# Sums of a pair's weights by GpSimd, one cut of 64 and 192 columns in every group, and two edits at the end, in a one-core encoder layer

## Chip, core and metric

The kernel runs on one core of one Trainium2 chip. Its time is the device time of one execution in microseconds (us); lower is better. The engines are TensorE (PE in the profile; its weight loads are listed apart as PEld), VectorE (DVE), ScalarE (ACT), GpSimd (POOL) and SyncE (SP), which here only issues transfers. Each engine works through its own queue in order and waits on semaphores for the others.

## The reference

One encoder layer over 512 positions of width 1024, all in float32: a feed-forward block, a mixing block (a Fourier mixer beside grouped-query attention), a second feed-forward block, and a last norm.

```
x = x + 0.5 * swiglu(rms_norm(x, ffn1_norm), ffn1_w_gate, ffn1_w_up, ffn1_w_down)
h = rms_norm(x, mix_norm);  u = h @ w_in
x = x + concatenate([fourier_mixer(u), gqa_attention(u)]) @ w_out
x = x + 0.5 * swiglu(rms_norm(x, ffn2_norm), ffn2_w_gate, ffn2_w_up, ffn2_w_down)
return rms_norm(x, final_norm)

swiglu(h, w_gate, w_up, w_down) = (silu(h @ w_gate) * (h @ w_up)) @ w_down
```

The feed-forward width is 2752: 21 chunks of 128 columns and a tail of 64. The change lies almost wholly in the two feed-forward blocks; its last two edits are in the end of the second one and in the final norm.

## The kernel before

**Precision.** Every float32 operand is split into a high part in the chip's reduced float32 format and a low part that is the rest: ScalarE casts the high part (`nc.scalar.copy`), VectorE subtracts it from the source (`lows`, line 121, where the profile has it as L122). A product is then three matmuls: high by high, high by low, low by high. `product` (line 158) issues these three where a full 512 columns, or a half of them, are the moving side.

**A feed-forward block** (`ffn`, line 254) takes its 21 chunks in four groups. For each group it first makes the activations and then multiplies them by the down weights (`down`, line 455), adding into x. The first group takes plain products. The three others use `seven` (line 375): the gate chunk and the up chunk of one index j are a *pair*, and the two matrix products of a pair, seen as a product of two by two blocks, are done with seven block products instead of eight. A block product is 12 matmuls with 256 moving columns (4 blocks of the contraction, three matmuls each), issued by `multiply` (line 381, matmul at L390), so a pair is 84 matmuls. In the two blocks there are 35 pairs in six such groups: 6, 6, 5, 6, 6 and 6.

**The weights of a pair** are prepared one pair ahead by `prepare` (line 334). SyncE loads the gate chunk into `raw_g` (2 buffers) and the up chunk into `raw_u` (3 buffers, shared with the raw down weights). With the quarters a11, a12 (in `raw_g`) and a21, a22 (in `raw_u`), each 128 by 512, four sums are formed by `combine` (line 361, L362): s1 = a21 + a22, s2 = s1 - a11, into the tile `s12`, and s3 = a11 - a21, s4 = a12 - s2, into `s34`. `s12` and `s34` have one buffer each. Then the raw gate chunk, `s12`, a22 and `s34` are split in high and low parts, which go into 128 by 1024 slots of one tile, `ring` (12 slots; 7 are used by a pair). A slot is taken again as soon as the block products that read it are done. The list that `prepare` returns is worked off in portions, after the steps of the pair before.

**The steps of a pair** in `seven`, with what follows each of them on other engines:

- step 0 writes the PSUM bank r; ScalarE copies r to p1 (L398)
- step 1 writes the bank p2; VectorE adds p1 (L411)
- step 9 of the pair before adds a22's product to that pair's r; ScalarE copies r (L434), VectorE multiplies by the gated half (L435), ScalarE and VectorE split the result into `at` (L436, L122)
- step 3 writes the bank q; ScalarE copies q to p5 (L398)
- step 4 adds to r, once p1 is copied; ScalarE copies r to u2 (L398)
- step 5 adds to q, once p5 is copied; VectorE adds u2 (L421), ScalarE applies the gate function (L422)
- step 6 adds to r, once u2 is copied; ScalarE copies r (L426), VectorE adds p5 (L427)

**Order.** In the feed-forward blocks the order of TensorE's and SyncE's instructions is the program's. The order on VectorE, ScalarE and GpSimd is chosen by the framework's scheduler when the program is built, and is fixed after that.

**Cut matmuls.** `CUTS` (line 33) names, for each group of `seven`, the matmuls (counted from the group's start) whose 256 columns are issued as two matmuls of fewer columns, with the same weights loaded twice:

```
CUTS = {
    (0, 1): {1: P}, (0, 2): {1: P, 2: P}, (0, 3): {4: P}, (2, 1): {1: HALF // 4}, (2, 2): {1: HALF - HALF // 4}, (2, 3): {2: P},
}
```

P is 128 and HALF is 256. The first number of a key is the block (0 is the first feed-forward block, 2 the second), the second the group.

**The end.** The last three of the eight output chunks of the second block's last group are done by `closing` (line 1280) in two halves of 256 columns (tiles `last`), so that the final norm of the first half can run under the products of the second. `finish` (line 1255) multiplies the chunks of x by the norm's row and sends them out: VectorE does six of the eight, GpSimd does chunks 2 and 3, and those two leave in one transfer issued by ScalarE's queue once both are multiplied. GpSimd otherwise only does small powers for norms, a few copies, and a few transfers.

Of the kernel before, what the change touches and what calls it, by code (L numbers as in the profile page):

```python
# [13 lines left out]
P = 128  # L14
S = 512
D = 1024
KD = D // P
F = 2752
NF = F // P
# [9 lines left out]
PLACES = 7  # L29
HALF = S // 2  # L30
USES = "a11", "a12", "s1", "s2", "s4", "s3", "a22"

CUTS = {
    (0, 1): {1: P}, (0, 2): {1: P, 2: P}, (0, 3): {4: P}, (2, 1): {1: HALF // 4}, (2, 2): {1: HALF - HALF // 4}, (2, 3): {2: P},
}
PIECES = (0, 2, 2, 0, 2, 1, 1)
KH = KD // 2
HI_DVE = ("f0", "f1")
SWAP_DMA = ("q1", "q2", "q3")

# [43 lines left out]
def encoder(ctx, tc, A, out):  # L84
    nc = tc.nc
# [43 lines left out]
        plain.append(plain.pop(i))  # L129
        return plain[-1]  # L130

    def weight_slots():
        return (slot().rearrange("p (a b) -> p a b", b=P) for _ in range(2))

    def raw_tile(src, name, n=KD):
        raw = wp.tile([P, KD, P], F32, tag="raw", name=f"raw_{name}")
# [5 lines left out]
        nc.scalar.activation(lo, asf(hi), AF.Copy, scale=-1.0)  # L142
        nc.gpsimd.dma_start(out=lo, in_=src, accum_op=ALU.add)

    def weights(src, name, n=KD, raw=None, by_dma=False):
        raw = raw or raw_tile(src, name, n)
        hi, lo = weight_slots()
        if name in HI_DVE:
            nc.vector.tensor_copy(hi[:, :n, :], raw[:, :n, :])
        else:  # L150
            nc.scalar.copy(hi[:, :n, :], raw[:, :n, :])  # L151
        if by_dma:
            rest_by_dma(lo, hi, src)
        else:
            lows(lo[:, :n, :], raw[:, :n, :], hi[:, :n, :])
        return hi, lo

    def product(ps, whi, wlo, mhi, mlo, first, last):
        nc.tensor.matmul(ps, whi, mhi, start=first, stop=False)  # L159
        nc.tensor.matmul(ps, whi, mlo, start=False, stop=False)  # L160
        nc.tensor.matmul(ps, wlo, mhi, start=False, stop=last)  # L161

    class Norm:
# [90 lines left out]
    def ffn(norm, after, wgu, wd, wdt, groups, opening, closing):  # L254
# [4 lines left out]
        n_ = norm.n  # L259
        n_plain = len(groups[0])  # L260
        with tc.tile_pool(name=f"act{n_}", bufs=1) as ap, tc.tile_pool(name=f"sums{n_}", bufs=2) as sp:
# [72 lines left out]
            def prepare(j, most=False):  # L334

                g = sp.tile([P, KD * P], F32, tag="raw_g", name=f"raw_g{n_}_{j}")
                u = wp.tile([P, KD * P], F32, tag="raw", name=f"raw_u{n_}_{j}")
                for t, c in ((g, 2 * j), (u, 2 * j + 1)):
                    nc.sync.dma_start(out=t.rearrange("p (a b) -> p a b", b=P), in_=wgu[c])
                a11, a12, a21, a22 = g[:, :S], g[:, S:], u[:, :S], u[:, S:]  # L340
                s12 = sp.tile([P, 2 * S], F32, tag="s12", bufs=1, name=f"s12_{n_}_{j}")
                s34 = sp.tile([P, 2 * S], F32, tag="s34", bufs=1, name=f"s34_{n_}_{j}")
                w = {}

                def both(names, src):
                    hi, lo = (take(most and names[0] != "a11") for _ in range(2))
                    nc.scalar.copy(hi, src)  # L347
                    lows(lo, src, hi)
                    for i, n in enumerate(names):
                        w[n] = tuple(t[:, i * S : (i + 1) * S] for t in (hi, lo))  # L350
                    w[max(names, key=USES.index), "slots"] = hi, lo

                def single(n, src):
                    t = take(False)
                    hi, lo = t[:, :S], t[:, S:]
                    nc.scalar.copy(hi, src)
                    lows(lo, src, hi)
                    w[n] = hi, lo
                    w[n, "slots"] = (t,)

                def combine(out, a, b, op):
                    nc.vector.tensor_tensor(out=out, in0=a, in1=b, op=op)  # L362

                return w, [
                    (both, ("a11", "a12"), g),
                    (combine, s12[:, :S], a21, a22, ALU.add),
                    (combine, s12[:, S:], s12[:, :S], a11, ALU.subtract),
                    (both, ("s1", "s2"), s12),
                    (single, "a22", a22),
                    (combine, s34[:, :S], a11, a21, ALU.subtract),  # L370
                    (combine, s34[:, S:], a12, s12[:, S:], ALU.subtract),
                    (both, ("s3", "s4"), s34),
                ]

            def seven(js, done, cuts):

                done = [done]
                banks = {}
                count = iter(range(84 * NF))

                def multiply(ps, wn, on, w, first):

                    (whi, wlo), (mhi, mlo) = w[wn], (part[on][:, i] for i in range(2))
                    for i in range(KH):
                        ks = slice(i * P, (i + 1) * P)
                        for o, (a, b) in enumerate(((whi, mhi), (whi, mlo), (wlo, mhi))):
                            cut = cuts.get(next(count), HALF)
                            for t in (slice(0, cut), slice(cut, HALF)):
                                if t.start < HALF:
                                    nc.tensor.matmul(  # L390
                                        ps[:, t], a[:, ks], b[:, i, t], start=first and i == 0 and o == 0,
                                        stop=i == KH - 1 and o == 2, skip_group_check=not first,
                                    )
                    give(*w.get((wn, "slots"), ()))

                def kept(ps, n, j):
# [58 lines left out]
            def down(d, group, gi):  # L455

                js = [j for j in group if j != "t"]
                whi, wlo = weights(wd[d][:, js[0] : js[-1] + 1, :], f"dn{n_}_{d}_{gi}", len(js))
                w = wt[d // 4][:, d % 4 * P : (d % 4 + 1) * P]

                def steps(ps, t):
                    for i, j in enumerate(group):
                        h, l = (at[:, where[j], o, t] for o in range(2))
                        first, last = i == 0, i == len(group) - 1
                        if j == "t":
                            nc.tensor.matmul(ps[:, t], w, h, start=first, stop=False)
                            nc.tensor.matmul(ps[:, t], w, l, start=False, stop=last)
                        else:
                            k = j - js[0]
                            product(ps[:, t], whi[:, k, :], wlo[:, k, :], h, l, first, last)  # L470
                        yield

                return steps
# [7 lines left out]
            for gi, group in enumerate(groups):  # L481
                last = gi == len(groups) - 1
                ahead = []
                if gi:
                    rest = seven(range(group[0] + 1, min(group[-1] + 2, NF)), ready, CUTS.get((n_, gi), {}))
# [769 lines left out]
    def finish(c0, c1, row, parts):  # L1255

        t = slice(c0 * P, c1 * P)
        pr = row(c0, c1)
        for ks in parts:
            block = slice(ks[0], ks[-1] + 1)  # L1260
            if ks[0] in by_pool:
                for k in ks:
                    nc.gpsimd.tensor_tensor(out=x[k][:, t], in0=x[k][:, t], in1=n3.rb[:, t], op=ALU.mult)
            else:
                y = xt[:, block, t]
                nc.vector.tensor_tensor(out=y, in0=y, in1=pr[:, t].unsqueeze(1).to_broadcast(list(y.shape)), op=ALU.mult)
            queue = nc.scalar if ks[0] in by_pool else nc.sync
            queue.dma_start(out=out[:, block, t], in_=xt[:, block, t])
# [170 lines left out]
```

## Time and profile before

| | us |
|---|---|
| median of 3 runs | 846.33 |
| lowest and highest | 846.12, 846.79 |
| the profiled execution's own time | 846.22 |
| its span, first to last instruction | 844.4 |
| mean granted TensorE clock | 0.997 |
| PE busy | 835.7 |
| DVE busy | 638.3 |
| ACT busy | 465.2 |
| POOL busy | 33.4 |

The profiled execution's time is 1.8 us longer than its span. In rows of groups, the columns are the line, the engine, the operation, what it writes and reads with shapes, the count, then after a bar the busy time in us and the mean of one in ns, then the idle time before. A matmul's end is modelled by the profiler, so the distance from start to start (or time over count in a stretch) tells the pace of matmuls better than their listed duration, which overlaps with the next.

### The profile page before, as it was taken

What the parts mean: (1) busy time and instruction counts of PE and PEld (TensorE: products, weight loads), DVE (VectorE), ACT (ScalarE), POOL (GpSimd) and SP (SyncE); (2) the same over time, 40 slices, a digit from 0 to 9 for tenths busy, and PEclk for the clock granted to TensorE, in tenths of its full rate; (3) what the DMA queues carried; (4) which work ended last, traced back from release to release, by engine and by line L of the source; (5) the groups of instructions that cost most, each with busy time, mean ns of one, the idle gap of its engine ahead of it and who ended that gap; (6) DMA issues with size and microseconds to landing.
All of it is one profiled execution on the core that took longest, in us unless ns stands there. A gap on an engine that the chain in (4) does not pass through costs nothing.

```text
span 844.4 us, 13712 instructions
## 1 busy us (share of the span) xinstructions
PE 835.7 (99%) x5441; PEld 756.4 (90%) x5441; DVE 638.3 (76%) x1007; ACT 465.2 (55%) x781; POOL 33.4 (4%) x35
## 2 busy tenths in 40 slices
PE   9999999999999999999999999999999999999996
PEld 6878998899989998889988888899989998899986
DVE  6997895489757847699998478999945895489453
ACT  7764664167424744677776347657632664157352
POOL 0110000000000000222000000100000000000002
PEclk9999999999999999999999999999999999999998
DMA  7664322323243123414110223543232322323213
GB/s 250 168 141 160 135 89 76 119 101 138 75 137 104 53 65 104 150 50 138 32 69 26 101 74 113 119 171 130 87 110 110 119 89 75 119 100 116 67 45 99
DMA packets 31424, 89.25 MB, mean 106 GB/s; under 512 B 3712, under 2 KB 9344, under 8 KB 31232
## 3 DMA queue, kind: packets, MB, share of 16 engines
q1 hardware_dynamic: 28320, 82.87, 29.0%
q0 software_dynamic: 2496, 4.99, 3.2%
q8 instruction: 42, 0.69, 0.3%
q10 hardware_dynamic: 544, 0.52, 0.2%
q14 instruction: 22, 0.18, 0.1%
HBM read 83.91 MB, written 2.10 MB: 102 GB/s over the span
## 4 chain that ended last, share of the span: by engine, by line
PE 97%; DVE 1%; DMA 0%; issue 0%; ACT 0%; POOL 0%; POOLq 0%; DVEq 0%; ACTq 0%
PE r L390 23%; PE q L390 11%; PE dn L161 8%; PE dn L160 8%; PE dn L159 8%; PE p L390 6%; PE mix L159 4%; PE mix L161 3%; PE mix L160 3%; PE gu L640 3%; PE gu L159 2%; PE gu L161 2%; PE gu L160 2%; PE mix L1130 2%; PE mix L1087 2%; PE mix L936 1%
## 5 line engine op out<-in xcount | busy, mean ns | idle before, releaser
L390 PE MATMUL r<-rt,ring 128*128 128x256 f32 x1687 | 211.1, 277 | 0.0
L390 PEld LDWEIGHTS r<-rt,ring 128*128 128x128 f32 x1687 | 201.9, 188 | 1.1
L161 PE MATMUL dn<-at,ring 128*128 128x512 f32 x300 | 116.9, 390 | 0.5 <-DVE ring L122 0.5
L160 PE MATMUL dn<-at,ring 128*128 128x512 f32 x300 | 116.8, 389 | 0.0
L159 PE MATMUL dn<-at,ring 128*128 128x512 f32 x300 | 116.7, 389 | 0.0
L390 PE MATMUL q<-rt,ring 128*128 128x256 f32 x840 | 107.2, 277 | 0.0
L476 DVE SCALAR_TENSOR_TENSOR gx<-dn,gx 128x512 f32<-128x512 f32 x61 | 42.1, 690 | 81.3 <-PE dn L161 81.3
L122 DVE TENSOR_TENSOR ring<-s,ring 128x1024 fp32r<-128x1024 f32 x70 | 85.5, 1222 | 21.2 <-ACT ring L347 12.6
L390 PEld LDWEIGHTS q<-rt,ring 128*128 128x128 f32 x840 | 101.0, 188 | 0.0
L151 ACT CAST ring<-raw_dn 128x768 fp32r<-128x768 f32 (+3 forms) x58 | 45.5, 788 | 91.7 <-PE dn L160 69.8
L347 ACT CAST ring<-s 128x1024 fp32r<-128x1024 f32 x70 | 73.0, 1051 | 24.8 <-PE p L390 11.2
L161 PEld LDWEIGHTS dn<-at,ring 128*128 128x128 f32 x300 | 56.3, 188 | 12.7 <-DVE ring L122 0.9
L159 PEld LDWEIGHTS dn<-at,ring 128*128 128x128 f32 x300 | 56.3, 188 | 11.3
L160 PEld LDWEIGHTS dn<-at,ring 128*128 128x128 f32 x300 | 56.3, 188 | 11.2
L122 DVE TENSOR_TENSOR ring<-raw_dn,ring 128x768 fp32r<-128x768 f32 (+3 forms) x58 | 51.7, 894 | 5.7 <-ACT ring L151 4.9
L390 PE MATMUL p<-rt,ring 128*128 128x256 f32 x420 | 53.6, 277 | 0.0
L122 DVE TENSOR_TENSOR ring<-raw_g,ring 128x1024 fp32r<-128x1024 f32 x35 | 42.8, 1222 | 11.7 <-PE p L390 10.5
L390 PEld LDWEIGHTS p<-rt,ring 128*128 128x128 f32 x420 | 50.5, 188 | 0.0
L347 ACT CAST ring<-raw_g 128x1024 fp32r<-128x1024 f32 x35 | 36.9, 1054 | 17.6 <-DMA raw_g<-in_wgu 10.6
L398 ACT COPY p<-r 128x256 f32<-128x256 f32 x35 | 13.0, 371 | 50.1 <-PE r L390 50.0
L422 ACT ACTIVATE g<-g 128x512 f32<-128x512 f32 x35 | 22.2, 633 | 19.0 <-DVE g L421 19.0
L228 POOL TENSOR_TENSOR r<-ms,mhalf 128x4 f32<-128x4 f32 (+1 forms) x5 | 5.9, 1181 | 669.4 <-DVE ms L221 669.4
(309 smaller groups left out, 1596.7 us busy)
## 6 DMA issues: line engine op xcount, KB each, us to landing
raw_g<-in_wgu SPq DMA_DIRECT2D x35, 512.0 KB, 3.7
raw_u<-in_wgu SPq DMA_DIRECT2D x35, 512.0 KB, 4.4
raw_dn<-in_wd SPq DMA_DIRECT2D x40, 384.0 KB, 3.0
raw_gu<-in_wgu SPq DMA_DIRECT2D x12, 512.0 KB, 3.5
raw_o<-in_wo SPq DMA_DIRECT2D x8, 512.0 KB, 3.4
raw_dn<-in_wd SPq DMA_DIRECT2D x8, 448.0 KB, 3.3
raw_wq<-in_wins SPq DMA_DIRECT2D x4, 512.0 KB, 4.1
raw_f<-in_winf SPq DMA_DIRECT2D x4, 512.0 KB, 3.5
```

The lines of the kernel that those rows point to most:

```text
L122: nc.vector.tensor_tensor(out=lo, in0=src, in1=asf(hi), op=ALU.subtract)
L151: nc.scalar.copy(hi[:, :n, :], raw[:, :n, :])
L159: nc.tensor.matmul(ps, whi, mhi, start=first, stop=False)
L160: nc.tensor.matmul(ps, whi, mlo, start=False, stop=False)
L161: nc.tensor.matmul(ps, wlo, mhi, start=False, stop=last)
L347: nc.scalar.copy(hi, src)
L390: nc.tensor.matmul(ps[:, t], a[:, ks], b[:, i, t], start=first and i == 0 and o == 0, stop=i == KH - 1 and o == 2, skip_group_check=not first,
L422: nc.scalar.activation(b["g"], b["g"], AF.Silu)
L476: nc.vector.scalar_tensor_tensor(out=x[d][:, t], in0=ps[:, t], scalar=0.5, in1=x[d][:, t], op0=ALU.mult, op1=ALU.add)
L640: nc.tensor.matmul(pss[c], w[:, k % 2, c], m[k], start=k == 0 and m is hh and w is hi, stop=k == KD - 1 and w is lo,)
L1087: nc.tensor.transpose(pts[n][:, c * P : (c + 1) * P], prob[t, b, c][:, kc * P : (kc + 1) * P], ident)
L1130: nc.tensor.matmul(outs[t, b], w, p, start=kc == 0 and i == 0, stop=kc == 3 and i == 1)
```

## The change

Four things are done.

1. `CUTS` goes. In each of the six groups of `seven`, the second matmul (index 1) is issued as 64 columns and then 192. Group 1 of the second block had exactly this before; the five others had other places or widths. The same cut is made in the second matmul of the first `last` product (the first half of output chunk 5).
2. The down weights of the last three output chunks are put 16 elements (64 bytes) further into their slots (`SKIP`).
3. `combine` issues its four sums of a pair to GpSimd instead of VectorE: 140 instructions of 128 by 512.
4. In `finish`, each of GpSimd's two chunks leaves by a transfer of its own right after its multiplication, instead of both in one. For the chunks that VectorE multiplies the transfer's source is written in another way and is the same.

The order of TensorE's instructions is otherwise unchanged. VectorE has 140 instructions fewer and keeps the order of most of the rest; GpSimd gets 140 more, in the order of the pairs, behind the transfers that it issues in each block's first group.

```diff
-CUTS = {
-    (0, 1): {1: P}, (0, 2): {1: P, 2: P}, (0, 3): {4: P}, (2, 1): {1: HALF // 4}, (2, 2): {1: HALF - HALF // 4}, (2, 3): {2: P},
-}
 PIECES = (0, 2, 2, 0, 2, 1, 1)
+SKIP = 16
+CUT = 1, P // 2
...
-    def weight_slots():
-        return (slot().rearrange("p (a b) -> p a b", b=P) for _ in range(2))
+    def weight_slots(n=KD, skip=0):
+        c = slice(skip, skip + n * P)
+        return (slot()[:, c].rearrange("p (a b) -> p a b", b=P) for _ in range(2))
...
+    def parts_of(n):
+
+        return (slice(0, CUT[1]), slice(CUT[1], HALF)) if n == CUT[0] else (slice(0, HALF),)
...
-    def product(ps, whi, wlo, mhi, mlo, first, last):
+    def product(ps, whi, wlo, mhi, mlo, first, last, cut=False):
         nc.tensor.matmul(ps, whi, mhi, start=first, stop=False)
-        nc.tensor.matmul(ps, whi, mlo, start=False, stop=False)
+        for t in parts_of(CUT[0]) if cut else (slice(0, ps.shape[-1]),):
+            nc.tensor.matmul(ps[:, t], whi, mlo[:, t], start=False, stop=False)
         nc.tensor.matmul(ps, wlo, mhi, start=False, stop=last)
...
                 def combine(out, a, b, op):
-                    nc.vector.tensor_tensor(out=out, in0=a, in1=b, op=op)
+                    nc.gpsimd.tensor_tensor(out=out, in0=a, in1=b, op=op)
...
-                            cut = cuts.get(next(count), HALF)
-                            for t in (slice(0, cut), slice(cut, HALF)):
-                                if t.start < HALF:
-                                    nc.tensor.matmul(
+                            for t in parts_of(next(count)):
+                                nc.tensor.matmul(
...
-                whi, wlo = weights(wd[d][:, js[0] : js[-1] + 1, :], f"dn{n_}_{d}_{gi}", len(js))
+                whi, wlo = weights(wd[d][:, js[0] : js[-1] + 1, :], f"dn{n_}_{d}_{gi}", len(js), skip=SKIP if closing and gi == len(groups) - 1 and d >= KD - 3 else 0)
...
-                            product(ps[:, t], whi[:, k, :], wlo[:, k, :], h, l, first, last)
+                            cut = first and d == KD - 3 and t == slice(0, HALF)
+                            product(ps[:, t], whi[:, k, :], wlo[:, k, :], h, l, first, last, cut)
...
                 for k in ks:
                     nc.gpsimd.tensor_tensor(out=x[k][:, t], in0=x[k][:, t], in1=n3.rb[:, t], op=ALU.mult)
+                    nc.scalar.dma_start(out=out[:, k, t], in_=x[k][:, t])
             else:
                 y = xt[:, block, t]
                 nc.vector.tensor_tensor(out=y, in0=y, in1=pr[:, t].unsqueeze(1).to_broadcast(list(y.shape)), op=ALU.mult)
-            queue = nc.scalar if ks[0] in by_pool else nc.sync
-            queue.dma_start(out=out[:, block, t], in_=xt[:, block, t])
+                nc.sync.dma_start(out=out[:, block, t], in_=y)
```

More of the change, by code (lines that the diff above doesn't have):

```diff
@@ L143, in rest_by_dma, with weights @@
         nc.gpsimd.dma_start(out=lo, in_=src, accum_op=ALU.add)
-    def weights(src, name, n=KD, raw=None, by_dma=False):
+    def parts_of(n):
+        return (slice(0, CUT[1]), slice(CUT[1], HALF)) if n == CUT[0] else (slice(0, HALF),)
+    def weights(src, name, n=KD, raw=None, by_dma=False, skip=0):
         raw = raw or raw_tile(src, name, n)
-        hi, lo = weight_slots()
+        hi, lo = weight_slots(n, skip)
         if name in HI_DVE:
@@ L373, in prepare, with seven @@
                 ]
-            def seven(js, done, cuts):
+            def seven(js, done):
                 done = [done]
                 banks = {}
-                count = iter(range(84 * NF))
+                count = iter(range(84 * len(js)))
                 def multiply(ps, wn, on, w, first):
@@ L386, in multiply @@
                         for o, (a, b) in enumerate(((whi, mhi), (whi, mlo), (wlo, mhi))):
-                            cut = cuts.get(next(count), HALF)
-                            for t in (slice(0, cut), slice(cut, HALF)):
-                                if t.start < HALF:
[L390 to L393, printed above, removed]
+                            for t in parts_of(next(count)):
+                                nc.tensor.matmul(
+                                    ps[:, t], a[:, ks], b[:, i, t], start=first and i == 0 and o == 0,
+                                    stop=i == KH - 1 and o == 2, skip_group_check=not first,
+                                )
                     give(*w.get((wn, "slots"), ()))
@@ L484, in ffn @@
                 if gi:
-                    rest = seven(range(group[0] + 1, min(group[-1] + 2, NF)), ready, CUTS.get((n_, gi), {}))
+                    rest = seven(range(group[0] + 1, min(group[-1] + 2, NF)), ready)
                 else:
```

## The prediction

> **What bounds the kernel now.** I read the page first: engine shares and the chain of work that ended last.
>
> ```profile
> span 844.4 us, 13712 instructions
> ...
> PE 835.7 (99%) x5441; PEld 756.4 (90%) x5441; DVE 638.3 (76%) x1007; ACT 465.2 (55%) x781; POOL 33.4 (4%) x35
> ...
> PE 97%; DVE 1%; DMA 0%; issue 0%; ACT 0%; POOL 0%; POOLq 0%; DVEq 0%; ACTq 0%
> ```
>
> TensorE is busy for 99% of the span and is 97% of the chain. Next, the view of waits, for TensorE alone:
>
> ```profile
> PE busy L579 <- DVE halves L609: 1.0, 1, 1.0
> PE rp L233 <- POOL r L228: 0.6, 1, 0.6
> PE dn L161 <- DVE ring L122: 0.5, 1, 0.5
> ```
>
> All its waits together are 2.1 us, and one of 0.5 us is for weights that VectorE was late with. So relieving VectorE can bring at most about 0.5 us. What is left to gain is the pace of the matmuls. Busy time by stretches, for the block products (columns: stretch and length, PE busy, PEld busy, clock, transfers): one pair; all of group 1 of the second block; all of its group 2.
>
> ```profile
> 86.43:95.95 9.52, 9.52 (x86) 9.52 (x85) 1.00 0.30 112
> 555.43:611.33 55.90, 55.90 (x493) 55.86 (x492) 1.00 0.32 109
> 645.40:703.45 58.05, 58.05 (x493) 58.01 (x492) 1.00 0.29 101
> ```
>
> A pair takes 9.52 us, 0.113 per matmul. The two groups have equal work, at the same granted clock, but group 2 takes 2.15 us more. The chain's rows show where: the first twelve products with the cut (13 matmuls), then a step of twelve, in group 1 and in group 2, and last the start of the first block's group 2, which has two cuts.
>
> ```profile
> 555.59 1.50 PE r L390 x13
> 557.09 1.36 PE p L390 x12
> ...
> 645.56 1.52 PE r L390 x13
> 647.08 1.41 PE p L390 x12
> ...
> 167.02 1.61 PE r L390 x14
> ```
>
> After the cut of 64 and 192 the steps run at 1.36 us; after the cut of 192 and 64 they stay at 1.41. The cut itself makes the first step 0.14 longer than 1.36.
>
> **The sums on GpSimd: what they need.** VectorE's work for a pair, in groups by shape (mean of one in ns after the busy time), and all L362 together:
>
> ```profile
> L122 DVE TENSOR_TENSOR ring<-s,ring 128x1024 fp32r<-128x1024 f32 x70 | 85.5, 1222 | 21.2 <-ACT ring L347 12.6 <-PE r L390 8.6
> L122 DVE TENSOR_TENSOR ring<-raw_g,ring 128x1024 fp32r<-128x1024 f32 x35 | 42.8, 1222 | 11.7 <-PE p L390 10.5 <-ACT ring L347 0.9
> L122 DVE TENSOR_TENSOR ring<-raw_u,ring 128x512 fp32r<-128x512 f32 x35 | 24.1, 688 | 2.4 <-PE r L390 0.9 <-ACT at L436 0.8 <-ACT g L422 0.2
> L435 DVE TENSOR_TENSOR u<-g,u 128x512 f32<-128x512 f32 x35 | 24.1, 687 | 10.4 <-ACT u L434 10.4
> L122 DVE TENSOR_TENSOR at<-u,at 128x512 fp32r<-128x512 f32 x35 | 24.1, 687 | 7.1 <-ACT at L436 7.1
> L427 DVE TENSOR_TENSOR u<-u,p 128x256 f32<-128x256 f32 x35 | 14.7, 421 | 1.2 <-ACT u L426 1.2
> ...
> 0.00:844.40 844.40, 93.94 (x140) 1.00 0.33 106
> ```
>
> The sums leave VectorE: 93.94 / 140 = 0.67 each, 2.7 us per pair. The six groups above stay, seven instructions per pair: 3 x 1.222 + 0.688 + 2 x 0.687 + 0.421 = 6.15 us. All seven read two operands from SBUF, as the sums do. Now the timeline, where GpSimd reads SBUF beside such an instruction and where it doesn't (start, length, instruction):
>
> ```profile
> 344.82 1.23 DVE L122 TENSOR_TENSOR ring<-raw_wq,ring 128x1024 fp32r<-128x1024 f32 x1
> 344.98 1.96 POOL L228 TENSOR_TENSOR r<-ms,mhalf 128x4 f32<-128x4 f32 x1 [295.92 <-DVE ms L221]
> ...
> 405.09 0.69 DVE L122 TENSOR_TENSOR qa<-rot_q,qa 64x512 fp32r<-64x512 f32 x1
> 405.21 1.03 POOL L1112 COPY zw<-z 128x512 f32<-128x512 f32 x1 [9.07 <-DVE z L1107]
> ...
> 426.10 0.64 DVE L1067 TENSOR_REDUCE mx<-mix 128x1 f32<-128x512 f32 x1
> 426.34 0.62 POOL L1112 COPY zw<-z 128x512 f32<-128x512 f32 x1 [20.09 <-PE mix L1087]
> ...
> 507.41 1.01 POOL L228 TENSOR_TENSOR r<-ms,mhalf 128x4 f32<-128x4 f32 x1 [49.98 <-DVE ms L221]
> ```
>
> The same power takes 1.01 us with VectorE idle and 1.96 beside a subtraction that ends at 346.05: 346.05 + 0.89 = 346.94, where the power ends. The same copy takes 0.62 beside a reduction out of PSUM and 1.03 beside a subtraction in SBUF. So GpSimd stands still until VectorE's two-operand instruction is over: the two share something that they can't use at once. I call it the port.
>
> How long a sum is on GpSimd is not in the trace; the nearest rows are these.
>
> ```profile
> 0.24 0.10 POOL L1427 MEMSET const-float32-0.0<- 128x1 f32 x1 [0.24 <-issue]
> ...
> 830.78 1.44 POOL L1263 TENSOR_TENSOR gx<-gx,rb 128x256 f32<-128x256 f32 x2 [1.24 <-ACT rb L241]
> ```
>
> A product of 128 by 256 takes 0.72. For 512 columns the bounds are 0.72 (no growth) and 1.44 (all of it grows). With 0.10 as the fixed part (the memset of one column) it is 0.10 + 2 x 0.62 = 1.34, which I take. Four sums are 5.36 us, and the port is wanted for 6.15 + 5.36 = 11.51 us per pair, where TensorE needs 9.52: 1.99 us too much. At the bounds it is 9.03 (fits) and 11.91 (2.39 too much). The sum needs no assumption on who yields: if VectorE never waited, GpSimd would have 9.52 - 6.15 = 3.37 us per pair for its 5.36. Only if a sum that has begun runs on beside VectorE is there room; the trace has no long GpSimd read that started first, so that is a rival.
>
> [...]
>
> **Where the lateness goes.** Behind a late sum stands ScalarE's cast of `s12` or `s34`, and behind that cast, in ScalarE's queue as built, the copies of p1, p5 and u2, and SyncE's later loads, since a `raw_g` buffer comes free with its last sum. How little the copies can wait:
>
> ```profile
> 82.63 1.36 PE q L390 x12
> 83.99 2.72 PE r L390 x24
> ...
> 79.83 1.23 DVE L122 TENSOR_TENSOR ring<-raw_g,ring 128x1024 fp32r<-128x1024 f32 x1 [2.05 <-PE p L390]
> ...
> 82.67 0.37 ACT L398 COPY u<-r 128x256 f32<-128x256 f32 x1 [0.54 <-PE r L390]
> 82.94 1.05 ACT L347 CAST ring<-s 128x1024 fp32r<-128x1024 f32 x1
> ```
>
> The u2 copy ends at 83.04 and the step on r that needs it starts at 83.99: 0.95 us. The weights themselves have more: the next pair's low part of `raw_g` is done at 81.06 and used from 83.99 + 1.36 = 85.35, 4.3 us later, but a slot can't be filled earlier than it is freed, so this slack doesn't grow.
>
> How many pairs carry the excess: the first pair of a group and the sums of the second are made in the down stage, where VectorE and GpSimd have room, which leaves 35 - 12 = 23. The second pair's subtractions and the next group's first sums, which stand in GpSimd's queue right behind, add up to six more: 29. I take the middle, 26: 26 x 1.99 = 52 us. Ends: 23 x 1.99 less the slack once per group, 46 - 6 x 4.3 = 20; and 29 x 2.39 = 69.
>
> **The cuts.** Group 2 of the second block gets the cut that group 1 has: -2.15 (its pairs would run at 1.36 a step where the port lets them). The others run at 1.36 already; the first block's group 2 loses its second cut, 1.61 to about 1.50 and one step less of transition: -0.1. For the last products (PE, PEld and VectorE's share of them):
>
> ```profile
> 818.68:828.03 9.35, 9.35 (x78) 9.30 (x77) 1.28 (x3) 1.00 0.01 2
> ```
>
> 78 matmuls in 9.35 are 0.120 each; at 0.1133 they take 8.84, and the cut 0.14: -0.37 if the quicker pace takes hold here. If it doesn't, the cut costs what it costs in the slow group, 1.52 - 1.41 = 0.11. The shift by 64 bytes is priced in none of the rows; it belongs to the same two ends. I take -0.2.
>
> **The two transfers.** From the timeline and the transfer view (KB each, median us to landing):
>
> ```profile
> 839.77 0.39 ACTq L1268 DMA_DIRECT2D out_y<-gx  x1
> ...
> out_y<-gx SPq DMA_DIRECT2D x5, 256.0 KB, 2.4
> out_y<-gx ACTq DMA_DIRECT2D x2, 256.0 KB, 3.0
> out_y<-gx SPq DMA_DIRECT2D x2, 128.0 KB, 1.8
> ```
>
> The last 256 KB leave at 839.77 and land 3.0 later. In two parts the first leaves some 0.7 earlier and the second is half as large. The other queue's last 256 KB then end it, so the gain lies between 0 (the same bytes are left to move) and 0.7; I take -0.3. The first half's transfers lie under products.
>
> **Sum.** 846.22 (this execution; its span plus 1.8; the runs' median is 846.33) + 52 - 2.15 - 0.1 - 0.2 - 0.3 = 895.5.
>
> **Rivals.** *First: GpSimd waits, but VectorE doesn't wait for it.* For: all rows with a wait have GpSimd waiting. Against: both then use the port at once. Each sum would wait at most 1.22 for a subtraction, 0.6 on average: 4 x 1.94 = 7.8 us per pair, under 9.52 and hidden. The cuts and the end are what is left: 846.2 - 2.75 = 843.5, faster. *Second: a sum is much shorter than 1.34.* At 0.95 the port is wanted for 9.95, 0.43 too much, 26 x 0.43 = 11 us, of which the slack of 4.3 per group swallows some or all: 844 to 855, I say 851. The price decides from 0.84 per sum on. For: the bound of 0.72. Against: GpSimd's product of 256 columns already takes that. *Third: the uniform cut doesn't bring the quick pace everywhere.* It has done so in one group of one program, and group 2's cut shows that a cut can fail. Each group lost costs 2.15; with GpSimd hidden and two more groups lost, while group 2 stays slow: 846.2 + 4.3 - 0.5 = 850.
>
> **Chances.** Forecast 0.73; first rival 0.14; second 0.09; third 0.04. Its own range is 846.2 + 20 - 2.7 = 863 to 846.2 + 69 - 2.7 = 913. With about a tenth of that case above 913 (waits of ScalarE at each hand-over, which I haven't priced), eight in ten need 848 to 922, which takes in the second and third rival and leaves the first out. Faster by over 0.2% (what a measurement here can tell from no change) is the first rival, 0.14; within 0.2% is the bottom of the second and third, 0.03; slower 0.83.
>
> **What would show it.** Right: L362's 140 instructions on GpSimd at 1.3 us or more each, longer where VectorE subtracts; VectorE's 1.22 rows lengthened or with idle time before them that no semaphore explains; a pair at 11 to 12 us from the third pair of a group on; TensorE waiting on ScalarE's copies. Wrong: a pair still at 9.52 with GpSimd at 4 x 1.9; then the first rival. The cuts: 1.36 a step in group 2 of the second block, 0.113 in the last products; where TensorE waits, only its stretches without a wait tell.

## The result and the profile after

| | before | after |
|---|---|---|
| median of the runs, us | 846.42 (846.12 to 846.79) | 887.10 (884.71 to 887.78) |
| ratio | | 1.0475, interval 1.046 to 1.049 |
| span of the profiled execution, us | 844.4 | 886.0 |
| mean granted TensorE clock | 0.997 | 0.990 |

The change makes the kernel 4.8% slower. The busy times on the changed kernel's page:

```profile
PE 848.6 (96%) x5441; PEld 762.7 (86%) x5441; DVE 642.6 (73%) x867; ACT 464.4 (52%) x781; POOL 268.3 (30%) x175
```

VectorE has 140 instructions fewer and is still busy 4 us longer: its other instructions have grown. TensorE, 99% busy before, now waits. Its waits (who waited <- for whom: us in total, times, longest):

```profile
PE q L392 <- ACT p L400: 14.3, 6, 2.6
PE r L392 <- ACT u L400: 9.4, 13, 1.2
PE r L392 <- ACT u L428: 2.9, 7, 1.0
PE dn L165 <- DVE ring L120: 2.8, 2, 1.9
```

26.6 of the 29.4 us shown are for ScalarE's copies of p5 (L400), u2 (L400) and r after step 6 (L428). The groups by shape, GpSimd's sums first, then VectorE's instructions that read two operands from SBUF (busy us, mean ns of one | idle before):

```profile
L366 POOL TENSOR_TENSOR s<-raw_g,s 128x512 f32<-128x512 f32 x35 | 70.6, 2017 | 0.9
L366 POOL TENSOR_TENSOR s<-raw_u 128x512 f32<-128x512 f32 x35 | 61.2, 1748 | 234.3 <-DMA raw_u<-in_wgu 159.8 <-issue 64.7 <-DVE ring L120 9.3
...
L120 DVE TENSOR_TENSOR ring<-s,ring 128x1024 fp32r<-128x1024 f32 x70 | 100.6, 1437 | 28.7 <-ACT ring L351 22.2 <-PE r L392 6.5
L120 DVE TENSOR_TENSOR ring<-raw_g,ring 128x1024 fp32r<-128x1024 f32 x35 | 57.7, 1648 | 16.7 <-PE p L392 12.4 <-issue 3.9 <-ACT ring L351 0.4
L120 DVE TENSOR_TENSOR ring<-raw_u,ring 128x512 fp32r<-128x512 f32 x35 | 37.8, 1079 | 2.5 <-ACT p L400 2.0
L429 DVE TENSOR_TENSOR u<-u,p 128x256 f32<-128x256 f32 x35 | 23.3, 667 | 1.3 <-ACT u L428 1.3
```

The three subtractions were 1222, 1222 and 688 ns before, the addition 421. The same shapes have grown by 18 to 58%, while the additions that take one operand from PSUM have kept their length (420 and 419 ns before, 415 and 416 now). So each side waits for the other. The first four sums of the first group, when VectorE does nothing of this kind, show what a sum takes alone:

```profile
73.89 1.31 POOL L366 TENSOR_TENSOR s<-raw_u 128x512 f32<-128x512 f32 x1 [9.32 <-DVE ring L120]
...
77.78 1.29 POOL L366 TENSOR_TENSOR s<-raw_g,s 128x512 f32<-128x512 f32 x1
```

Where the time went: the six groups of block products, by stretches (stretch and length, PE busy, PEld busy, clock, transfers). First the sum of the six in the kernel before, then two of the six of the changed kernel and the sum of its six:

```profile
sum 328.39, PE 328.38 PEld 328.00; mean PE 54.73 PEld 54.67
```

```profile
78.12:142.12 64.00, 59.94 (x493) 59.02 (x492) 0.95 0.27 91
176.19:237.94 61.75, 57.27 (x493) 56.44 (x492) 1.00 0.27 94
...
sum 367.67, PE 341.09 PEld 335.40; mean PE 56.85 PEld 55.90
```

39.3 of the 41.6 us by which the span grew are in these groups. Within a group the pairs are not alike. For the first group, its second to fifth pair, from one step 1 to the next:

```profile
87.78:97.36 9.58, 9.58 (x86) 9.58 (x85) 1.00 0.30 111
97.36:108.28 10.92, 10.10 (x86) 9.70 (x85) 1.00 0.30 106
108.28:124.43 16.15, 12.92 (x87) 12.43 (x85) 0.79 0.22 76
124.43:133.97 9.54, 9.54 (x87) 9.54 (x86) 1.00 0.32 97
```

A pair was 9.52 before. One loses 1.4 us, one loses 6.6 (part of it with a lower granted clock, which comes back at the end of this document), and the others next to nothing.

### The profile page after: what moved, and what is told of

The parts are those of the page before. It is cut to its first block, busy times and chain, and to the rows that moved or that the text cites. A ratio compares the mean times of both kernels' runs of the same rounds, so it can differ in the third digit from the quotient of the medians.

```text
span 886.0 us, 13818 instructions
## 1 busy us (share of the span) xinstructions
PE 848.6 (96%) x5441; PEld 762.7 (86%) x5441; DVE 642.6 (73%) x867; ACT 464.4 (52%) x781; POOL 268.3 (30%) x175
## 4 chain that ended last, share of the span: by engine, by line
PE 82%; DVE 7%; issue 4%; ACT 3%; DMA 1%; POOL 1%; SPq 0%; DVEq 0%; POOLq 0%; ACTq 0%
PE r L392 18%; PE dn L165 8%; PE dn L162 8%; PE dn L164 8%; PE q L392 7%; PE p L392 4%; DVE ring L120 3%; PE mix L162 3%; PE mix L165 3%; PE mix L164 3%; PE gu L162 2%; PE gu L165 2%; PE gu L164 2%; DVE u L437 2%; PE mix L1133 2%
## 5 line engine op out<-in xcount | busy, mean ns | idle before, releaser
L392 PE MATMUL r<-rt,ring 128*128 128x256 f32 x1686 | 218.4, 283 | 12.2 <-ACT u L400 9.4
L392 PEld LDWEIGHTS r<-rt,ring 128*128 128x128 f32 x1686 | 206.7, 192 | 17.4 <-ACT u L400 12.1
L366 POOL TENSOR_TENSOR s<-raw_u 128x512 f32<-128x512 f32 x35 | 61.2, 1748 | 234.3 <-DMA raw_u<-in_wgu 159.8
L120 DVE TENSOR_TENSOR ring<-s,ring 128x1024 fp32r<-128x1024 f32 x70 | 100.6, 1437 | 28.7 <-ACT ring L351 22.2
L366 POOL TENSOR_TENSOR s<-raw_g,s 128x512 f32<-128x512 f32 x35 | 70.6, 2017 | 0.9
L120 DVE TENSOR_TENSOR ring<-raw_g,ring 128x1024 fp32r<-128x1024 f32 x35 | 57.7, 1648 | 16.7 <-PE p L392 12.4
L120 DVE TENSOR_TENSOR ring<-raw_dn,ring 128x768 fp32r<-128x768 f32 (+3 forms) x58 | 56.3, 973 | 16.3 <-ACT ring L154 15.1
L366 POOL TENSOR_TENSOR s<-raw_g,raw_u 128x512 f32<-128x512 f32 x35 | 50.9, 1454 | 50.9 <-DVE ring L120 50.9
L366 POOL TENSOR_TENSOR s<-s,raw_g 128x512 f32<-128x512 f32 x35 | 54.2, 1548 | 1.8
```

Of the source, the lines that this page charges most:

```text
L120: nc.vector.tensor_tensor(out=lo, in0=src, in1=asf(hi), op=ALU.subtract)
L366: nc.gpsimd.tensor_tensor(out=out, in0=a, in1=b, op=op)
L392: nc.tensor.matmul(ps[:, t], a[:, ks], b[:, i, t], start=first and i == 0 and o == 0, stop=i == KH - 1 and o == 2, skip_group_check=not first,
```

## The experiments

Times are medians; the ratio is to the kernel before on the same chip, with its 95% interval. e8, e9 and e11 were run once each.

### e1: the sums back on VectorE

```diff
-                    nc.gpsimd.tensor_tensor(out=out, in0=a, in1=b, op=op)
+                    nc.vector.tensor_tensor(out=out, in0=a, in1=b, op=op)
```

> The changed kernel with its four sums per pair back on VectorE; everything else as changed. If the sums are the whole loss (first theory: VectorE's instructions with two operands in SBUF and GpSimd's reads of SBUF exclude each other, both ways), what is left are the cuts and the end: 846.4 - 2.15 - 0.1 - 0.37 - 0.3 = 843.5 us. If part of the +41 us came from the cuts or the end (a rival: the uniform cut loses the quick pace when nothing waits, 2.15 us for each group lost), the time is above 846.

Measured: 843.52 us, ratio 0.9969 (0.9957 to 0.998). The sums are the whole loss, and 887.1 - 843.5 = 43.6 us is their price. The cuts and the end together bring 2.8 us, about what they were priced at (which part brought what is told further on). Two groups of this kernel, the first block's and the second block's group 2:

```profile
167.09:222.99 55.90, 55.90 (x493) 55.86 (x492) 1.00 0.31 104
645.59:701.49 55.90, 55.90 (x493) 55.86 (x492) 1.00 0.31 105
```

### e2: the sums on GpSimd alone, in the kernel before

```diff
-                    nc.vector.tensor_tensor(out=out, in0=a, in1=b, op=op)
+                    nc.gpsimd.tensor_tensor(out=out, in0=a, in1=b, op=op)
```

> The kernel before with its four sums per pair on GpSimd, and nothing else of the change. If the parts of the change add up, this is the changed kernel's 887.1 plus the 2.9 us that the cuts and the end bring: 890. If TensorE's waits swallow the slow pace of the second block's group 2 (there are 5 to 6 us of waits in each group that a slower step could fill), it is 887 to 888. A rival in which the new cuts make the waits worse gives clearly less than 885.

Measured: 888.13 us, ratio 1.0483 (1.0464 to 1.0502), between the first two expectations and too near to both to choose.

### e3 and e4: GpSimd works beside VectorE, and nobody needs its results

Both are e1 with this in the preparation of a pair; e3 has the multiplication, e4 the memset in the loop:

```diff
+            scr = sp.tile([P, 480], F32, tag="scr", bufs=1, name=f"scr{n_}")
...
+                def idle(src):
+                    nc.gpsimd.tensor_tensor(out=scr[:, :1], in0=scr[:, :1], in1=src[:, :1], op=ALU.add)
+                    for _ in range(4):
+                        nc.gpsimd.tensor_tensor(out=scr, in0=scr, in1=scr, op=ALU.mult)
```

> As e1 (sums on VectorE), and for each pair GpSimd does one multiplication of one column that reads s1 and then four multiplications of 128 by 480 on a tile of its own that nobody else reads. VectorE's and ScalarE's orders are those of e1, so nobody waits for GpSimd's result. First theory (the two exclude each other in SBUF, both ways): the four take 4 x 1.22 us alone (1.30 x 480 / 512), VectorE's seven subtractions and products and its four sums take 6.15 + 2.68, together 13.7 us per pair against TensorE's 9.52: VectorE's instructions with two SBUF operands are lengthened to 1.5 us and more, and the time is 880 to 970. Rival (what costs in the change is that ScalarE and VectorE get the sums late, from a slower engine through one more hand-over): nobody gets anything late here, VectorE's instructions keep 0.69 and 1.22 us and the time is e1's, 843.5.

> As e3, but GpSimd's four instructions are memsets of the same 128 by 480 tile: they write SBUF and read nothing there. If the exclusion is with GpSimd's reads alone, VectorE keeps 0.69 and 1.22 us and the time is e1's, 843.5 (within 0.5). If any access of GpSimd to SBUF shuts VectorE out, VectorE is lengthened by the memsets' own time (to be read from their row) and the time lies between e1 and e3, above 850.

Measured: e3 911.38 us, ratio 1.0767 (1.0753 to 1.0782); e4 843.71 us, ratio 0.9967 (0.9954 to 0.998), the time of e1. Groups of e3, then of e4:

```profile
L375 POOL TENSOR_TENSOR scr<-scr 128x480 f32<-128x480 f32 x140 | 207.2, 1480 | 11.0
...
L370 DVE TENSOR_TENSOR s<-s,raw_g 128x512 f32<-128x512 f32 x35 | 37.3, 1065 | 0.2
...
L438 DVE TENSOR_TENSOR u<-u,p 128x256 f32<-128x256 f32 x35 | 31.2, 891 | 1.4 <-ACT u L437 1.3
```

```profile
L375 POOL MEMSET scr<- 128x480 f32 x140 | 70.0, 500 | 8.1
...
L370 DVE TENSOR_TENSOR s<-s,raw_g 128x512 f32<-128x512 f32 x35 | 24.1, 688 | 0.2
L438 DVE TENSOR_TENSOR u<-u,p 128x256 f32<-128x256 f32 x35 | 14.7, 421 | 1.2 <-ACT u L437 1.2
```

The orders of the other engines are the same in e1, e3 and e4. With GpSimd's multiplications reading SBUF, VectorE's instructions with two SBUF operands grew, an addition of 421 ns to 891 on the mean; with its memsets, which only write, they kept the lengths of e1 (421 and 688). So lengthened VectorE instructions alone cost 67.9 us here (911.4 against e1's 843.5), without any sum coming from GpSimd.

### e5 and e6: two or three of the four sums on GpSimd

```diff
-                    nc.gpsimd.tensor_tensor(out=out, in0=a, in1=b, op=op)
+                    (nc.gpsimd if a is a11 or a is a21 else nc.vector).tensor_tensor(out=out, in0=a, in1=b, op=op)
```

(e6: the condition `a is not a12`.)

> The changed kernel with two of the four sums of a pair on GpSimd (s1 and s3) and two on VectorE (s2 and s4). What the two engines want of the shared access is 6.15 + 2 x 0.69 + 2 x 1.30 = 10.13 us per pair, 0.61 over TensorE's 9.52. If that excess builds up over the five pairs that follow the first of a group and only what goes over the weights' slack of 4.3 us is lost, 5 x 0.61 = 3.05 is swallowed: 843.5 to 846. If the slack doesn't come off, as in the prediction's sum (26 pairs times the excess): 843.5 + 16 = 859. If each sum on GpSimd costs alike, whatever the sum of the two engines (half of e1's distance to the changed kernel): 865.

> The changed kernel with three of the four sums on GpSimd (s1, s2 and s3) and s4 on VectorE. Wanted of the shared access: 6.15 + 0.69 + 3 x 1.30 = 10.74, 1.22 over 9.52. With the slack taken off once per group: 6 x (5 x 1.22 - 4.3) = 11, so 854, and up to 3 more where the clock falls after a wait. Without slack: 843.5 + 26 x 1.22 = 875. Each sum alike: three quarters of 43.6, 876.

Measured: e5 867.7 us, ratio 1.0251 (1.0234 to 1.0268); e6 883.05 us, ratio 1.0438 (1.0409 to 1.0467). Two sums cost 24 us, three 39.5, four 43.6. The sum over what both engines want of the shared access fails, with the slack taken off (844, 854) and without (859, 875). The third figure for e5, 865, is near, but that for e6, 876, is not: the loss does not go by the number of sums either. So the question after these runs was what, if not the two engines' total, sets the loss.

### e7 and e12: no step of TensorE waits for ScalarE's copies

```diff
-                        multiply(b["r"], "s2", "t2", w, False)
+                        b["r"] = bank(f"r4{n_}_{j}")[:, :HALF]
+                        multiply(b["r"], "s2", "t2", w, True)
...
-                        multiply(b["q"], "s4", "b22", w, False)
+                        b["q"] = bank(f"q5{n_}_{j}")[:, :HALF]
+                        multiply(b["q"], "s4", "b22", w, True)
...
-                        multiply(b["r"], "s3", "t3", w, False)
+                        b["r"] = bank(f"r6{n_}_{j}")[:, :HALF]
+                        multiply(b["r"], "s3", "t3", w, True)
```

e12 does the same in step 9 (`r9`).

> The changed kernel, but steps 4, 5 and 6 each start a PSUM bank of their own instead of adding to r or q, so TensorE waits for no copy of p1, p5 or u2 (left out of the result: the earlier products in r and q). The orders on VectorE, GpSimd and TensorE stay. If the lateness reaches TensorE through those copies only, and the weights have slack left (in the changed kernel no step waited for weights), most of the 31.6 us of waits and the slow matmuls behind them go: 850 to 862. If the two engines' excess is what counts and TensorE only met it at the copies first, the waits come back at the weights' low parts (TensorE waiting for VectorE's L120) and the time stays at 875 to 887.

> As e7, and step 9 too has a PSUM bank of its own, so that TensorE waits for none of ScalarE's copies (left out of the result: all sums over several block products of a pair but one). The orders on all engines are those of e7. If what costs is that a sum comes late for a cast behind which those copies stand in ScalarE's queue, the 17.2 us that e7 still waited for the copy of step 6 go as well: 848 to 858. If VectorE and GpSimd together can't keep pace with TensorE (6.15 + 0.84 for VectorE's reads of PSUM + 5.2, 11.3 to 12.2 us per pair against 9.52; five pairs a group; slack 4.3), TensorE comes to wait for VectorE's low parts instead, and 29 to 54 us are lost: 872 or more.

Measured: e7 872.83 us, ratio 1.031 (1.0295 to 1.0326); e12 854.34 us, ratio 1.0099 (1.0084 to 1.0114). e7 fell between its two expectations because step 9 still waited for the copy after step 6 (L431 there):

```profile
PE r L392 <- ACT u L431: 17.2, 18, 2.0
```

In e12 that wait is gone too. Two of its six groups and the sum, and then its groups by shape:

```profile
78.72:134.62 55.90, 55.90 (x493) 55.86 (x492) 1.00 0.29 99
...
562.36:619.40 57.04, 56.19 (x493) 55.96 (x492) 1.00 0.29 103
...
sum 327.01, PE 326.15 PEld 325.74; mean PE 54.36 PEld 54.29
```

```profile
L366 POOL TENSOR_TENSOR s<-raw_g,s 128x512 f32<-128x512 f32 x35 | 71.6, 2044 | 0.9
...
L120 DVE TENSOR_TENSOR ring<-s,ring 128x1024 fp32r<-128x1024 f32 x70 | 104.3, 1490 | 16.1 <-ACT ring L351 11.8 <-PE r L392 4.1 <-issue 0.3
```

This sum and the subtractions for `s12` and `s34` are even longer than in the changed kernel (2017 and 1437), and TensorE runs its groups as if nothing were wrong: 327.0 us for the six, against 367.7. VectorE and GpSimd together can keep TensorE's pace within a group. The loss reached TensorE through the copies, 887.1 - 854.3 = 32.8 of the 43.6 us. The rest, 10.8, lies outside the groups but for 0.9 (327.0 against e1's 326.1): there this kernel's products with the down weights wait 7.6 us for VectorE.

### e13: the sums late, without contention

```diff
-                    nc.gpsimd.tensor_tensor(out=out, in0=a, in1=b, op=op)
+                    nc.vector.tensor_tensor(out=out, in0=a, in1=b, op=op)
+                    if b is a11 or b is not a11 and a is a12:
+                        c = out[:, :1]
+                        nc.gpsimd.tensor_tensor(out=scr[:, :1], in0=scr[:, :1], in1=c, op=ALU.mult)
+                        for _ in range(1):
+                            nc.gpsimd.memset(scr, 0.0)
+                        nc.gpsimd.tensor_tensor(out=c, in0=c, in1=scr[:, :1], op=ALU.add)
```

> As e1 (sums on VectorE), but between s2 and the cast of s12, and between s4 and the cast of s34, GpSimd reads one column, does one memset of 128 by 480 (which took nothing from VectorE in e4) and adds the zero that it left to one column: the casts get their sums some 1.8 us later (0.6 + 0.5 + 0.6 and the hand-overs), about as much later as GpSimd's two sums made them in the changed kernel, and VectorE has next to nothing to share its access with. If lateness alone is the cause, the time is most of the way to the changed kernel: 870 to 885, with TensorE waiting for the copies of p5 and u2. If the exclusion with its lengthened instructions is needed, the margins of about 1 us take up most of it: 844 to 855.

Measured: 849.58 us, ratio 1.0035 (1.0021 to 1.0049). GpSimd's three instructions before each cast take 0.52 + 0.50 + 0.67 us by their rows, VectorE's keep 0.69 and 1.22, and the delay costs 6.1 us over e1, a seventh of 43.6. But ScalarE's queue has another order here. In the traces of e1 and of the changed kernel the cast of `s34` stands ahead of the copy of p5 in 12 of the 35 pairs; in e13 it does so in none. In the first group's fourth pair the copy of p5 goes first, and the cast, which waits for GpSimd, comes later:

```profile
110.65 0.37 ACT L408 COPY p<-q 128x256 f32<-128x256 f32 x1
...
112.89 1.05 ACT L353 CAST ring<-s 128x1024 fp32r<-128x1024 f32 x1 [1.22 <-POOL s L374]
```

So e13 shows that late sums cost little where their cast does not hold up that copy. What the same delay would cost without contention in the changed kernel's order was not tried.

Of e13's loss, the one listed wait of TensorE is 1.7 us. Much of the rest is pace. In five of the six groups, behind a hitch of some 0.1 us in step 5 of the fourth pair, the steps take 1.41 us instead of 1.36, in four of them to the end of the group. That is the pace that the second block's group 2 had in the kernel before. Two steps after the hitch, from the first group:

```profile
115.42 1.58 PE L400 MATMUL p<-rt,ring 128*128 128x256 f32 x12
116.83 1.58 PE L400 MATMUL r<-rt,ring 128*128 128x256 f32 x12
```

### e8 and e9: the last products

e8 is e1 with `SKIP = 0`; e9 is e1 with `cut = False` in `down`.

> e1 without the shift of the last down weights by 64 bytes. If the pace of the last products comes from the cut, the first half of the last three chunks takes 8.98 us as in the changed kernel; if the shift matters, up to 9.35. Time 843.5 to 843.9.

> e1 without the cut in the first of the last products, with the shift. If the cut sets the pace, the first half of the last three chunks goes back to 9.35 us (0.120 a matmul), and the time to 843.9; if the shift sets it, it is 8.8 to 9.0.

Measured: 844.06 and 843.59 us in one run each, which says nothing at this size; the stretches do. The first half of the last three chunks in e1, in e8, in e9 (before: 9.35):

```profile
816.68:825.66 8.98, 8.98 (x79) 8.94 (x78) 1.28 (x3) 1.00 0.01 2
```

```profile
816.39:825.84 9.45, 9.45 (x79) 9.40 (x78) 1.28 (x3) 1.00 0.01 2
```

```profile
816.43:825.62 9.19, 9.19 (x78) 9.14 (x77) 1.27 (x3) 1.00 0.01 2
```

Neither is what was expected: e8 lies above its bounds, e9 between its two. The cut without the shift gains nothing and costs its 0.1. The shift alone gives 0.16, both together 0.37. This repeats: the stretch takes 8.98 in all ten traces that have both, and 9.35 in the two that have neither (before and e2). Over both halves, from the first start to the last, it is 15.63 us before, 15.73 in e8, 15.21 in e9 and 15.18 in e1, so there nearly all of the gain comes with the shift. But e4, with both, takes 15.02, its second half 0.17 less than e1's, so these two edits are not all that decides the pace.

### e11: TensorE made to wait, with the sums on VectorE as in e1

```diff
                     nc.scalar.copy(t, ps)
+                    if n == "p5" and j == js[3]:
+                        for _ in range(AGAIN[n_, js[0]]):
+                            nc.scalar.copy(t, ps)
```

> As e1, but in the fourth pair of each group ScalarE repeats the copy of p5 6, 8, 9, 10, 12 and 15 times (first to last group), so TensorE waits before step 5 by some 1.5, 2.3, 2.7, 3.1, 3.9 and 5.1 us (0.4 a copy less 1.0 of margin), with VectorE and GpSimd as in e1. If the granted clock of 0.50 that the changed kernel showed in two groups comes from TensorE's wait itself, it appears here too, behind the longer waits, for some 3 us with matmuls at 0.213 us instead of 0.113; a wait near 2.9 may have it or not, and the longest must have it. If it came from the other engines' contention, all matmuls here run at 0.113. Time: 843.5 plus the six waits of about 18.6, plus 2.8 for each group with the slow clock: 862 to 875.

Measured: 882.16 us in one run. The waits came out longer than meant, 24.0 us in all, and the slow clock came in all six groups, so the time is above the range. VectorE's subtractions and addition keep 1.22 and 0.42 us; its order differs from e1's in a few places. What it tells is in the last section.

## Why the prediction was right, and where it was not

**What bounds the kernel, and the gain from VectorE.** Right as far as the runs go: e1 relieves VectorE of nothing, has no listed wait of TensorE in its groups, and gains its 2.8 us by the pace of the matmuls alone.

**The exclusion.** Right, and it holds both ways, so the first rival (GpSimd waits, VectorE doesn't) falls. A piece of the changed kernel's timeline (start, length, instruction) shows both directions, and the rest of the chain:

```profile
108.17 1.99 DVE L120 TENSOR_TENSOR ring<-s,ring 128x1024 fp32r<-128x1024 f32 x1
...
110.23 1.42 POOL L366 TENSOR_TENSOR s<-raw_g,raw_u 128x512 f32<-128x512 f32 x1 [1.16 <-DVE ring L120]
...
111.10 1.63 DVE L120 TENSOR_TENSOR ring<-s,ring 128x1024 fp32r<-128x1024 f32 x1 [0.62 <-ACT ring L351]
...
111.61 2.27 POOL L366 TENSOR_TENSOR s<-raw_g,s 128x512 f32<-128x512 f32 x1
...
112.66 2.30 DVE L120 TENSOR_TENSOR ring<-raw_g,ring 128x1024 fp32r<-128x1024 f32 x1
113.91 1.04 ACT L351 CAST ring<-s 128x1024 fp32r<-128x1024 f32 x1 [2.05 <-POOL s L366]
...
116.07 0.37 ACT L400 COPY p<-q 128x256 f32<-128x256 f32 x1
...
116.50 2.21 PE L392 MATMUL q<-rt,ring 128*128 128x256 f32 x12 [2.61 <-ACT p L400]
```

The sum that starts at 111.61 finds a subtraction that ends at 112.73, and ends 1.15 later. The subtraction that starts at 112.66 finds that sum, which ends at 113.88, and itself ends at 114.96, 1.08 later.

**The length of a sum.** Right: 1.34 us were taken, 1.29 to 1.31 are seen alone. The second rival (0.95) falls.

**The sum of 11.51 us per pair against 9.52, and 26 pairs at 1.99: wrong.** This is the step that failed, in two ways. First, whole durations were counted as exclusive. The two pairs of rows above show that 1.08 of a subtraction's 1.22 and 1.15 of a sum's 1.30 are: 0.14 or 0.15 of each passed under the other. Over all such collisions of this trace the end lies 1.08, 0.55 and 0.28 us after GpSimd's for VectorE's instructions of 1.22, 0.69 and 0.42, and 1.15 after VectorE's for 95 of GpSimd's sums. With these lengths the pair wants 3 x 1.08 + 3 x 0.55 + 0.28 + 4 x 1.15 = 9.77 us, 0.25 too much instead of 1.99, which five pairs and 4.3 us of slack can bear. Second, the total was taken for what sets the time. e5, e6 and e12 show that it is not: two sums on GpSimd fit with room to spare (3 x 1.08 + 5 x 0.55 + 0.28 + 2 x 1.15 = 8.57) and cost 24 us; all four with the copies out of TensorE's way cost nothing in the groups but 0.9 us. The sign that went with the sum, a pair at 11 to 12 us from the third of a group on, did not come either: the pairs shown above take 9.58, 10.92, 16.15 and 9.54.

**Where the lateness goes: right, and it is most of the mechanism** (32.8 of the 43.6 us, by e12). The prediction named the path (late sum, cast of `s34`, behind it in ScalarE's queue the copies) and a margin of 0.95 us, but priced the loss by the total. The same piece of the pair in e1, where ScalarE's order from the cast of `s34` to the copy of p5 is the same:

```profile
104.62 1.23 DVE L120 TENSOR_TENSOR ring<-s,ring 128x1024 fp32r<-128x1024 f32 x1 [0.26 <-PE r L392]
...
107.30 0.69 DVE L366 TENSOR_TENSOR s<-raw_g,s 128x512 f32<-128x512 f32 x1
...
110.30 0.39 ACT L400 COPY p<-q 128x256 f32<-128x256 f32 x1
...
111.26 1.52 PE L392 MATMUL q<-rt,ring 128*128 128x256 f32 x12
```

Step 1 of this pair starts at 105.82 in e1 and at 108.28 in the changed kernel; counted from there, the subtraction that frees `s34` ends at 0.03 against 1.88, the last sum at 2.17 against 5.60, and the copy of p5 starts at 4.48 against 7.79, 3.31 later. In e1 the copy is done 0.57 before TensorE needs it; what goes over that is TensorE's wait of 2.61. Of the 3.43 us by which the last sum is late, 1.24 is GpSimd's longer time for two sums, 0.97 is this sum stopped by the subtraction ahead of it (2.27 instead of 1.30), 0.77 the subtraction before stopped by a sum (1.99 instead of 1.22), and the rest, 0.45, is a balance: that subtraction starts 1.09 later, and 0.78 is saved because other work of VectorE no longer stands between it and the sums. The framework also orders ScalarE's queue differently when the sums change engine: the cast of `s12` stands ahead of the copy of p1 in 2 of the 35 pairs in e1 and in 12 in the changed kernel. What that alone costs was not tried.

**The forecast.** 895.5 was made as 52 for the sums less 2.75; the sums cost 43.6 and the rest brought 2.8. The 52 is near only because two errors met: an excess eight times too large, and no loss from a path that was described and not priced.

**The cuts and the end.** Group 2 of the second block gained its 2.15 (58.05 to 55.90) and the first block's group 2 its 0.1 (56.02 to 55.90), so the third rival falls. The first half of the last products gained 0.37, the good end of the bounds, but not by the cut alone, to which the prediction gave it: that gains nothing without the shift of 64 bytes (e8), and the shift alone brings 0.16 (e9). The two transfers were priced at 0.3 and gained nothing: from the copy of the norm's row to the end of the span it is 6.5 us before (844.4 - 837.88) and 6.6 in e1 (842.0 - 835.43). The row before, and that of e1:

```profile
837.88 0.37 ACT L251 COPY rb<-rp 128x256 f32<-128x256 f32 x1 [1.84 <-PE rp L233]
```

```profile
835.43 0.37 ACT L255 COPY rb<-rp 128x256 f32<-128x256 f32 x1 [1.83 <-PE rp L237]
```

**The better version.** e1, the change without its sums, beats both kernels: 0.31% faster than before (0.2 to 0.43%).

## What to carry to other kernels

Before moving work to GpSimd, list VectorE's instructions with two SBUF operands around it: in the changed kernel each collision stopped the one that came second until the first was done, for all but 0.14 or 0.15 us of its own length. A total that fits under the bound was not enough: e5's 8.57 us against 9.52 cost 24. Follow the late result through every in-order queue that it passes, and compare the delay with the margin of whatever stands behind it there, most of all the small copies that the bounding engine waits for.

## What the runs showed of the hardware

**The granted clock fell to half after long waits of TensorE, and each row of matmuls at that clock took another 1.2 to 2.7 us.** In the changed kernel two of the six groups have a clock of 0.95. Stretches of the first: ahead of the wait of 2.6 us before step 5, shortly after it, and from the next wait on (in the next pair, shown above, the clock is 1.00 again).

```profile
108.28:113.60 5.32, 5.32 (x49) 5.32 (x48) 1.00 0.15 57
...
117.00:119.00 2.00, 1.71 (x10) 1.41 (x9) 0.59 0.65 177
119.33:124.20 4.87, 4.87 (x23) 4.87 (x24) 0.50 0.22 90
```

At 0.50 a matmul takes 4.87 / 23 = 0.21 us instead of 0.113. e11 has no contention and shows the same behind its longest wait:

```profile
804.60:808.00 3.40, 3.40 (x16) 3.40 (x17) 0.50 0.00 0
```

So the wait alone was enough there. Over the groups of eight of these kernels (the changed one, e2, e3, e5, e6, e7, e11 and e13), counted as the distance from one matmul's start to the next: of 17 gaps of 1.5 to 2.2 us none was followed by a row of matmuls at half the clock; of 20 gaps of 2.2 to 3.0 us six were, and two more after a further gap of 1.5 us; of 11 gaps above 3.4 us all were. The matmuls of such a row take 1.2 to 2.7 us more than at 0.113.

Why some gaps of the middle kind were followed by the half clock and others not, these runs do not show: in the changed kernel there are four of 2.89 or 2.90 us, and two were (those before 116.50 us and, after a further gap of 1.48, before 713.33 us) and two not (before 214.59 and 811.65 us).

The clock may also be why the runs of a kernel with such waits spread: e6's go from 880.63 us at a mean clock of 0.994 to 886.96 at 0.990. No run tests that.

In the changed kernel the six groups take 41.6 us more than in e1. By the starts of the matmuls, 31.6 of it are gaps of over 0.3 us, 7.6 are matmuls of 0.18 us or more behind such gaps, and 2.3 the pace of 1.41 us a step, into which some streams fall behind a gap, as in e13.

**The pace of the last products' matmuls changed with the place of their weights.** A shift of the last down weights by 64 bytes within their slots took 0.16 us off 9.35 without any cut (e9), and only with it did the cut bring 0.113 us a matmul in the first half (8.98 in e1 against 9.45 in e8). Why the address matters was not tried.
